# Seven-product up-projection of a gated MLP: the order of the products on TensorE, written out or left to the scheduler

## The chip, the cores and the metric

The kernel runs on one core of a Trainium2 chip, in one launch. Its time is device microseconds (us) of that core from start to end. Three runs of the kernel before gave 2424.66, 2425.37 and 2426.58 us; the median, 2425.37 us, is the time before. Five engines have instruction queues of their own and run side by side: TensorE (PE, matrix products into the accumulator PSUM), VectorE (DVE), ScalarE (ACT), GpSimd (POOL) and SyncE (SP, which here issues the DMA transfers). PSUM has eight banks; a product of 128 x 512 fp32 results fills one.

## What is computed

A two-layer decoder trunk on one sequence of 1024 positions and 1024 features. Each layer has a mixer (a gated recurrence with a state-space layer in layer 0, latent attention in layer 1) and then a gated MLP, which the change is about:

```python
def conv_ffn(hn, w_in, conv_w, conv_b, w_out):
    a, u = jnp.split(hn @ w_in, 2, axis=-1)       # w_in: 1024 x 5632
    a = causal depthwise convolution of width 3 over the positions of a, + conv_b
    return (jax.nn.silu(a) * u) @ w_out           # w_out: 2816 x 1024
```

`h = h + conv_ffn(rmsnorm(h))` is done once in each of the two layers. Everything is fp32; each fp32 matrix product is made of three products of halves (high x high, high x low, low x high).

## The kernel before

`ffn` works on 22 *pairs*: pair f is 128 columns of the `a` half and the 128 columns of the `u` half that belong to them. For one pair the product of `w_in` with the normed activations is a 2 x 2 block problem: two halves of the 1024 input features, two halves of the columns (u and a), two halves of the positions (`lo`, `hi`, 512 each). Instead of eight block products it makes seven, with sums of blocks before and after (Winograd's form). The seven are called by their weight operand: `a11`, `a12`, `s1`, `s2`, `s3`, `a22`, `s4`. A product is 12 matmuls of 128 x 512 (four steps of the inner dimension, three half products each, lines 161 to 163). The activations' blocks and their sums (`b11`, `b21`, `b22`, `bt1` to `bt4`) are made once per layer.

A pair has three PSUM banks. X takes `a11` and then, added to it, `a12`; Y takes `s2`, then `s3`, then `a22`, each added to what is there; Z takes `s1`, then `s4`. Between two products on one bank its contents are read: after `a11` ACT copies X to `p1` (line 895); after `s2` DVE writes `p16 = p1 + Y` (901); after `s3` DVE writes the `hi` half of the convolution's input, `ax = p1 + Y` (906), to which POOL adds `p5` (907); after `s1` ACT copies Z to `p5` (911); after `a22` DVE writes the `lo` half of `ax` (915), and then the convolution runs on DVE (1058, twice 1060) and SiLU on ACT (1061). The next product on that bank waits for the read. `tail` ends a pair: `p16 += Z` (922) and `ct[lo] *= X` (923) on DVE, `ct[hi] *= p16` on POOL (924), and a DMA of `ct` to DRAM. After all pairs `down` multiplies by `w_out`; its matmuls write tiles called `row`.

The weights of a pair come by DMA (846) into `raw` tiles (room for two pairs). POOL forms the sums `s1`, `s3`, `s2`, `s4` (877, 879, 881, 883), and `operand` splits each of the seven into a high half (ACT, line 129, `op`) and a low half (DVE, line 130, `op`). The `op` tiles are a ring of six; the text prepares each product three steps ahead (`LOOK`), so a slot is free again when the product six places earlier has ended.

Numbers of buffers matter below: `p16` has one, `p5` two, `p1` three, `ax` one, `ct` two. X, Y and Z of pairs 3 on are dealt from a ring of the eight banks; pair 2's Z is bank 0, which was pair 0's X.

What sets the order: each engine runs its own queue strictly in order. The order in the queues is made at build time by a scheduler that simulates the program and takes from the text, engine by engine, what it reckons to be ready first. So the list `steps` in the text is a proposal: products can be moved and interleaved on TensorE by the scheduler, and before the change they are.

Of the kernel before, what the change touches and what calls it, by code (L numbers as in the profile page):

```python
# [20 lines left out]
P = 128  # L21
# [35 lines left out]
class Trunk:  # L57
# [101 lines left out]
    def mm3(self, out, l, r, start, stop, **how):  # L159
        mm = self.nc.tensor.matmul  # L160
        mm(out, l[0], r[0], start=start, stop=False, **how)  # L161
        mm(out, l[0], r[1], start=False, stop=False, **how)  # L162
        mm(out, l[1], r[0], start=False, stop=stop, **how)  # L163
# [657 lines left out]
    def ffn(self, L, h, pool, final=None):  # L821
# [11 lines left out]
        KH = KD // 2  # L833
        quad = [P, 2, KH, HALF]
# [20 lines left out]
        def product(bank, w, x, start):  # L855

            for k in range(KH):
                self.mm3(
                    bank, [w[:, i, k] for i in range(2)], [v[:, k] for v in x],
                    start and k == 0, k == KH - 1, skip_group_check=not start,  # L860
                )

        class Pair:


            def __init__(s, f, r):
                s.f, s.r, s.op = f, r, {}
# [21 lines left out]

        def run(p, name):  # L890
# [7 lines left out]
            elif name == "s2":  # L898
                product(p.Y, o, B["t2"], True)
                p.p16 = piece("p16", 1)  # L900
                V.tensor_tensor(out=p.p16, in0=p.p1, in1=p.Y, op=ALU.add)  # L901
            elif name == "s3":
                product(p.Y, o, B["t3"], False)
                p.ax = pool.tile([P, S + 2], F32, tag="ax", name="ax", bufs=1)
                G.memset(p.ax[:, 0:2], 0.0)
                V.tensor_tensor(out=p.ax[:, 2 + HALF:], in0=p.p1, in1=p.Y, op=ALU.add)
                G.tensor_tensor(out=p.ax[:, 2 + HALF:], in0=p.ax[:, 2 + HALF:], in1=p.p5, op=ALU.add)
            elif name == "s1":
                product(p.Z, o, B["t1"], True)
                p.p5 = piece("p5", 2)  # L910
                ACT.activation(p.p5, p.Z, AF.Copy)  # L911
            elif name == "a22":
                product(p.Y, o, B["t4"], False)
                p.ct = pool.tile([P, S], F32, tag="ct", name="ct")
                V.tensor_tensor(out=p.ax[:, 2:2 + HALF], in0=p.p1, in1=p.Y, op=ALU.add)
                self.conv(p.ct, p.ax, taps, p.f, slice(0, S))
            else:
                product(p.Z, o, B["22"], False)
# [21 lines left out]
        def second_rows(t, q, ps):  # L940
            cols = slice(t * P, (t + 1) * P)
            if q == 0:
                f1 = B["f1"] = kn(piece("p16", 1))
# [54 lines left out]
        for p, y, z in zip(early, (5, 6, 7), (3, 4, 0)):  # L998
            p.banks = {"Y": y, "Z": z}
        steps = [(pairs[f], n) for f, n in (  # L1000
            (0, "s1"), (1, "s1"), (0, "s4"), (1, "s4"), (0, "s2"), (0, "s3"), (0, "a22"), (1, "s2"), (1, "s3"),
            (1, "a22"), (2, "s1"), (2, "s2"), (2, "s4"), (2, "s3"), (3, "a11"), (2, "a22"), (3, "s2"),
        )]
        order = ("a11", "s2", "a12", "s1", "s3", "a22", "s4")
# [565 lines left out]
```

## Time and profile before

| | us |
|---|---|
| median of three runs | 2425.37 |
| the profiled execution, its own time | 2429.82 |
| its span from the first to the last instruction | 2428.1 |
| up-projection stage of layer 0, first to last matmul of its products | 462.2 to 968.3 |
| the same of layer 1 | 1673.9 to 2180.0 |

The trace lists every instruction with its start, its duration and, in brackets, how long its engine had been idle before it and whose end it waited for. Times are us from the span's start. A matmul's listed duration is longer than the distance to the next one, because matmuls are pipelined; the pace of TensorE is read from starts. Tile names come without numbers: `au` is any of the banks X, Y, Z; `b` and `bt` are the blocks of the activations (`bt` belongs to `s1`, `s2`, `s3` and `a22`; `b` to `a11`, `a12` and `s4`); `p` is `p1`, `p5` or `p16`, told apart by line.

### The profile page before, as it was taken

The page shows a single profiled execution, that of the slowest core. Times are in us where ns is not written, and L with a number is a line of the kernel's source. Part 1 is how long each engine was busy: PE and PEld are TensorE (multiplying, and loading weights), DVE is VectorE, ACT ScalarE, POOL GpSimd, SP SyncE. Part 2 cuts the span into 40 slices and gives each one's busy share as a digit, 9 for nine tenths or more (in the row PEclk, how much of TensorE's full clock was granted, in tenths as well). Part 3 has the DMA queues.
Part 4 walks back from the last instruction along what each step waited for, and adds up shares of the span by engine and source line. Part 5 has one row for each costly group of instructions (what it writes and reads, how often), then busy time and mean ns, then how long its engine had stood idle before and what let it go on. Part 6 is the DMA issues. An engine that isn't in the chain of part 4 may idle for free.

```text
span 2428.1 us, 29242 instructions
## 1 busy us (share of the span) xinstructions
PE 2287.5 (94%) x10945; PEld 1862.1 (77%) x10945; DVE 1575.4 (65%) x2627; ACT 862.6 (36%) x1498; POOL 563.5 (23%) x509
## 2 busy tenths in 40 slices
PE   7999999989999999999989999999889999999997
PEld 6777878767777777888888888887667777778886
DVE  6878886775666666644467777847656666666435
ACT  4454553532332322311233555635322323223102
POOL 0465310233444342000001000001334443320000
PEclk9999999999999999999999999999999999999999
DMA  6333324122221223432301001431222222234211
GB/s 187 121 103 89 100 82 167 60 61 70 78 79 61 78 70 113 165 105 68 108 10 43 29 31 37 149 127 45 61 75 73 78 65 74 79 110 172 96 39 70
DMA packets 196309, 208.05 MB, mean 86 GB/s; under 512 B 28288, under 2 KB 152392, under 8 KB 195656
## 3 DMA queue, kind: packets, MB, share of 16 engines
q1 hardware_dynamic: 196168, 206.19, 26.0%
q8 instruction: 86, 1.41, 0.2%
q14 instruction: 55, 0.45, 0.1%
HBM read 165.39 MB, written 39.58 MB: 84 GB/s over the span
## 4 chain that ended last, share of the span: by engine, by line
PE 70%; DVE 13%; issue 7%; POOL 5%; DMA 3%; ACT 2%; SPq 0%; POOLq 0%; DVEq 0%; ACTq 0%
PE row L162 9%; PE row L163 9%; PE row L161 9%; PE au L161 7%; PE au L162 7%; PE au L163 7%; DVE op L130 2%; POOL ct L924 2%; POOL raw L879 2%; DMA raw<-in_ffn_w_in 1%; PE ptps L1468 1%; DVE wlo L130 1%; DVE p L901 1%; PE tt L162 1%; PE tt L163 1%
## 5 line engine op out<-in xcount | busy, mean ns | idle before, releaser
L161 PE MATMUL au<-bt,op 128*128 128x512 f32 x704 | 287.2, 408 | 60.6 <-DVE p L901 39.2
L129 ACT ACTIVATE op<-raw 128x512 fp32r<-128x512 f32 x260 | 162.7, 629 | 479.1 <-PE au L163 245.5
L129 ACT ACTIVATE whi<-raw 128x1024 fp32r<-128x1024 f32 (+4 forms) x143 | 143.4, 1004 | 410.5 <-PE row L163 273.5
L130 DVE TENSOR_TENSOR op<-raw,op 128x512 fp32r<-128x512 f32 x260 | 260.0, 1003 | 43.7 <-ACT op L129 38.2
L162 PE MATMUL au<-bt,op 128*128 128x512 f32 x704 | 282.2, 401 | 0.9 <-DVE bt L130 0.9
L162 PE MATMUL row<-wlo,g 128*128 128x512 f32 x704 | 275.7, 392 | 0.4 <-DVE wlo L130 0.2
L163 PE MATMUL au<-bt,op 128*128 128x512 f32 x704 | 275.3, 400 | 0.0
L163 PE MATMUL row<-whi,g 128*128 128x512 f32 x704 | 272.2, 390 | 0.0
L161 PE MATMUL row<-whi,g 128*128 128x512 f32 x704 | 265.7, 393 | 0.2 <-ACT whi L129 0.2
L130 DVE TENSOR_TENSOR wlo<-raw,whi 128x1024 fp32r<-128x1024 f32 (+4 forms) x143 | 173.2, 1212 | 109.8 <-ACT whi L129 107.8
L161 PE MATMUL au<-b,op 128*128 128x512 f32 x528 | 213.3, 404 | 28.9 <-ACT p L911 25.2
L1082 DVE TENSOR_TENSOR h<-h,row 128x512 f32<-128x512 f32 x192 | 129.5, 685 | 163.2 <-PE row L163 162.8
L161 PEld LDWEIGHTS au<-bt,op 128*128 128x128 f32 x704 | 134.8, 192 | 110.6 <-DVE p L901 55.0
L162 PE MATMUL au<-b,op 128*128 128x512 f32 x528 | 208.8, 395 | 0.0
L163 PE MATMUL au<-b,op 128*128 128x512 f32 x528 | 203.0, 396 | 0.0
L877 POOL TENSOR_TENSOR s<-raw 128x512 f32<-128x512 f32 x44 | 67.9, 1545 | 548.0 <-DMA raw<-in_ffn_w_in 420.7
L163 PEld LDWEIGHTS au<-bt,op 128*128 128x128 f32 x704 | 134.9, 192 | 32.2
L162 PEld LDWEIGHTS au<-bt,op 128*128 128x128 f32 x704 | 135.1, 192 | 31.8 <-DVE bt L130 1.5
L162 PEld LDWEIGHTS row<-wlo,g 128*128 128x128 f32 x704 | 132.2, 188 | 30.1 <-DVE wlo L130 2.1
L161 PEld LDWEIGHTS row<-whi,g 128*128 128x128 f32 x704 | 131.9, 188 | 30.1 <-ACT whi L129 1.5
L163 PEld LDWEIGHTS row<-whi,g 128*128 128x128 f32 x704 | 132.2, 188 | 29.7
L161 PEld LDWEIGHTS au<-b,op 128*128 128x128 f32 x528 | 99.5, 188 | 67.9 <-ACT p L911 41.3
(596 smaller groups left out, 4898.4 us busy)
## 6 DMA issues: line engine op xcount, KB each, us to landing
raw<-in_ffn_w_in SPq DMA_DIRECT2D x176, 256.0 KB, 3.3
g_dram<-ct SPq DMA_DIRECT2D x44, 512.0 KB, 4.0
raw<-in_ffn_w_out SPq DMA_DIRECT2D x44, 512.0 KB, 3.4
raw<-in_even_w_in SPq DMA_DIRECT2D x40, 512.0 KB, 3.9
gr<-g_dram SPq DMA_DIRECT2D x40, 512.0 KB, 4.5
h<-in_x SPq DMA_DIRECT2D x16, 512.0 KB, 10.4
raw<-in_even_w_out SPq DMA_DIRECT2D x16, 512.0 KB, 3.7
raw<-in_odd_w_out SPq DMA_DIRECT2D x16, 512.0 KB, 3.7
```

Of the source, the lines that this page charges most:

```text
L129: nc.scalar.activation(hi, src, AF.Copy)
L130: nc.vector.tensor_tensor(out=lo, in0=src, in1=hi.bitcast(F32), op=ALU.subtract)
L161: mm(out, l[0], r[0], start=start, stop=False, **how)
L162: mm(out, l[0], r[1], start=False, stop=False, **how)
L163: mm(out, l[1], r[0], start=False, stop=stop, **how)
L877: tt(out=s.s1, in0=p("a21"), in1=p("a22"), op=ALU.add)
L879: tt(out=p("s3"), in0=p("a11"), in1=p("a21"), op=ALU.subtract)
L901: V.tensor_tensor(out=p.p16, in0=p.p1, in1=p.Y, op=ALU.add)
L924: G.tensor_tensor(out=ct[:, hi], in0=ct[:, hi], in1=p.p16, op=ALU.mult)
L1082: nc.vector.tensor_tensor(out=part, in0=part, in1=acc, op=ALU.add)
L1468: nc.tensor.transpose(ps[:, w:w + P], pb[q][:, kk * P:(kk + 1) * P], self.ident)
```

## The change

Three edits, all in `ffn`. First, `product` is put under `issue_after(last)`: each product may be issued on TensorE only after the last matmul of the product before it in the text, so TensorE takes the products whole and in the order of `steps`. Second, that order is rewritten: `s1` and `s3` change places in the repeated `order` (now `a11 s2 a12 s3 s1 a22 s4`), and the list for the first pairs is mixed, so that between two products on one bank there is one on another. Third, `p16` gets a second buffer, and the `hi` half of the convolution's input is formed in another way: DVE writes `p1 + Y` to a tile of its own, `u3`, and POOL writes `ax = u3 + p5` once both are there (`second`), where before DVE wrote into `ax` and POOL added to it in place. The number of instructions and DMAs is the same.

```diff
--- before.py
+++ after.py
@@ -1,5 +1,5 @@
 import math
-from contextlib import ExitStack, contextmanager
+from contextlib import ExitStack, contextmanager, nullcontext
 
 import numpy as np
 
@@ -160,7 +160,7 @@
         mm = self.nc.tensor.matmul
         mm(out, l[0], r[0], start=start, stop=False, **how)
         mm(out, l[0], r[1], start=False, stop=False, **how)
-        mm(out, l[1], r[0], start=False, stop=stop, **how)
+        return mm(out, l[1], r[0], start=False, stop=stop, **how)
 
     def rstd(self, ss, n, width):
 
@@ -831,6 +831,7 @@
         g_row = self.gain(self.a["norm_ffn_g"][L:L + 1])
         g_dram = tc.dram_tile([NF, P, S], F32, name="g_dram")
         KH = KD // 2
+        last = []
         quad = [P, 2, KH, HALF]
         piece = lambda name, bufs: pool.tile([P, HALF], F32, tag=name, name=name, bufs=bufs)
         kn = lambda x: x.rearrange("p (k n) -> p k n", k=KH)
@@ -854,17 +855,19 @@
 
         def product(bank, w, x, start):
 
-            for k in range(KH):
-                self.mm3(
-                    bank, [w[:, i, k] for i in range(2)], [v[:, k] for v in x],
-                    start and k == 0, k == KH - 1, skip_group_check=not start,
-                )
+            with tc.issue_after(last[0].ins) if last else nullcontext():
+                for k in range(KH):
+                    mm = self.mm3(
+                        bank, [w[:, i, k] for i in range(2)], [v[:, k] for v in x],
+                        start and k == 0, k == KH - 1, skip_group_check=not start,
+                    )
+            last[:] = [mm]
 
         class Pair:
 
 
             def __init__(s, f, r):
-                s.f, s.r, s.op = f, r, {}
+                s.f, s.r, s.op, s.p5, s.u3 = f, r, {}, None, None
 
             def part(s, name):
                 j, i = {"a11": (0, 0), "a21": (0, 1), "a12": (1, 0), "a22": (1, 1), "s2": (0, 0), "s3": (0, 1), "s4": (1, 0)}[name]
@@ -887,6 +890,13 @@
 
         lo, hi = slice(0, HALF), slice(HALF, S)
 
+        def second(p):
+
+            if p.p5 is not None and p.u3 is not None:
+                p.ax = pool.tile([P, S + 2], F32, tag="ax", name="ax", bufs=1)
+                G.memset(p.ax[:, 0:2], 0.0)
+                G.tensor_tensor(out=p.ax[:, 2 + HALF:], in0=p.u3, in1=p.p5, op=ALU.add)
+
         def run(p, name):
             o = p.op.pop(name, None)
             if name == "a11":
@@ -897,18 +907,18 @@
                 product(p.X, o, B["21"], False)
             elif name == "s2":
                 product(p.Y, o, B["t2"], True)
-                p.p16 = piece("p16", 1)
+                p.p16 = piece("p16", 2)
                 V.tensor_tensor(out=p.p16, in0=p.p1, in1=p.Y, op=ALU.add)
             elif name == "s3":
                 product(p.Y, o, B["t3"], False)
-                p.ax = pool.tile([P, S + 2], F32, tag="ax", name="ax", bufs=1)
-                G.memset(p.ax[:, 0:2], 0.0)
-                V.tensor_tensor(out=p.ax[:, 2 + HALF:], in0=p.p1, in1=p.Y, op=ALU.add)
-                G.tensor_tensor(out=p.ax[:, 2 + HALF:], in0=p.ax[:, 2 + HALF:], in1=p.p5, op=ALU.add)
+                p.u3 = piece("u3", 1)
+                V.tensor_tensor(out=p.u3, in0=p.p1, in1=p.Y, op=ALU.add)
+                second(p)
             elif name == "s1":
                 product(p.Z, o, B["t1"], True)
                 p.p5 = piece("p5", 2)
                 ACT.activation(p.p5, p.Z, AF.Copy)
+                second(p)
             elif name == "a22":
                 product(p.Y, o, B["t4"], False)
                 p.ct = pool.tile([P, S], F32, tag="ct", name="ct")
@@ -940,7 +950,7 @@
         def second_rows(t, q, ps):
             cols = slice(t * P, (t + 1) * P)
             if q == 0:
-                f1 = B["f1"] = kn(piece("p16", 1))
+                f1 = B["f1"] = kn(piece("p16", 2))
                 V.tensor_tensor(out=f1, in0=kn(ps), in1=f11[:, :, cols], op=ALU.subtract)
                 return
             V.tensor_tensor(out=f2[:, :, cols], in0=kn(ps), in1=B["f1"], op=ALU.subtract)
@@ -998,10 +1008,10 @@
         for p, y, z in zip(early, (5, 6, 7), (3, 4, 0)):
             p.banks = {"Y": y, "Z": z}
         steps = [(pairs[f], n) for f, n in (
-            (0, "s1"), (1, "s1"), (0, "s4"), (1, "s4"), (0, "s2"), (0, "s3"), (0, "a22"), (1, "s2"), (1, "s3"),
-            (1, "a22"), (2, "s1"), (2, "s2"), (2, "s4"), (2, "s3"), (3, "a11"), (2, "a22"), (3, "s2"),
+            (0, "s1"), (1, "s1"), (0, "s4"), (0, "s2"), (1, "s4"), (0, "s3"), (1, "s2"), (0, "a22"), (1, "s3"),
+            (2, "s1"), (1, "a22"), (2, "s2"), (2, "s4"), (2, "s3"), (3, "a11"), (2, "a22"), (3, "s2"),
         )]
-        order = ("a11", "s2", "a12", "s1", "s3", "a22", "s4")
+        order = ("a11", "s2", "a12", "s3", "s1", "a22", "s4")
         steps += [(pairs[3], n) for n in order[2:]] + [(p, n) for p in pairs[4:] for n in order]
 
         def prep(p, name):
```

What the scheduler makes of it is seen in three places of layer 0's repeated part. Line numbers in `ffn` are 1 to 10 higher after the change.

TensorE before, one turn of the repeated part; the first matmul of each product (or of a piece of one). `au` with a number is one use of a bank: 5270 is Y of a pair n, 4992 is Y of pair n-1, 5170 is Z of pair n-1, 5249 is X of pair n and 5388 is X of pair n+1.

```order
L161 MATMUL au_4992<-bt3_4498,op_4986 128x512
...
L161 MATMUL au_5270<-bt2_4107,op_5205 128x512
...
L161 MATMUL au_5170<-bt1_4106,op_5107 128x512
...
L161 MATMUL au_4992<-bt4_4501,op_5007 128x512
...
L163 MATMUL au_5170<-bt1_4106,op_5107 128x512
...
L161 MATMUL au_5170<-b22_4108,op_5161 128x512
...
L161 MATMUL au_5249<-b21_4102,op_5226 128x512
...
L161 MATMUL au_5388<-b11_4101,op_5324 128x512
```

In turn: `s3` of n-1, `s2` of n, `s1` of n-1 with `a22` of n-1 inside it, `s4` of n-1 right behind that `s1` on the same bank, `a12` of n, `a11` of n+1.

TensorE after, one turn; X, Y and Z of one pair are 5258, 5276 and 5333.

```order
L161 MATMUL au_5258<-b11_4101,op_5189 128x512
...
L161 MATMUL au_5276<-bt2_4107,op_5211 128x512
...
L161 MATMUL au_5258<-b21_4102,op_5232 128x512
...
L161 MATMUL au_5276<-bt3_4498,op_5252 128x512
...
L161 MATMUL au_5333<-bt1_4106,op_5273 128x512
...
L161 MATMUL au_5276<-bt4_4501,op_5291 128x512
...
L161 MATMUL au_5333<-b22_4108,op_5306 128x512
```

All seven products of the turn belong to one pair, whole, and no two neighbours share a bank.

GpSimd before, one turn; `raw` 5303 and 5306 are the weights of pair n+1, 5442 and 5445 those of pair n+2, `ct_5359` is pair n's product-to-be.

```order
L877 TENSOR_TENSOR s1_5545<-raw_5442,raw_5445 128x512
L883 TENSOR_TENSOR raw_5306<-raw_5306,raw_5303 128x4x128
L905 MEMSET ax_5479 128x2
L879 TENSOR_TENSOR raw_5442<-raw_5442 128x4x128
L924 TENSOR_TENSOR ct_5359<-ct_5359,p16_5283 128x512
L881 TENSOR_TENSOR raw_5442<-s1_5545,raw_5442 128x4x128
L907 TENSOR_TENSOR ax_5479<-ax_5479,p5_5461 128x512
```

GpSimd after, one turn; pair n has `ax_5348`, `raw` 5309 and 5312 are those of pair n+2.

```order
L880 TENSOR_TENSOR s1_5395<-raw_5309,raw_5312 128x512
L882 TENSOR_TENSOR raw_5309<-raw_5309 128x4x128
L886 TENSOR_TENSOR raw_5172<-raw_5172,raw_5169 128x4x128
L898 TENSOR_TENSOR ax_5348<-u3_5327,p5_5346 128x512
L897 MEMSET ax_5488 128x2
L934 TENSOR_TENSOR ct_5366<-ct_5366,p16_5289 128x512
L884 TENSOR_TENSOR raw_5309<-s1_5395,raw_5309 128x4x128
```

Before, `ct *= p16` (924) stands behind `s1` and `s3` of a pair whose weights have just been loaded (877, 879). After, it (934) stands ahead of these two (880, 882), behind the adding up of `ax` and the clearing of its two first columns.

VectorE before, from the `lo` half of pair n's `ax` (5340) on; `p16_5422` is that of the pair behind it.

```order
L915 TENSOR_TENSOR ax_5340<-p1_5262,au_5270 128x512
L130 TENSOR_TENSOR op_5403<-raw_5164,op_5403 128x512
L1058 TENSOR_SCALAR ct_5359<-ax_5340,taps_4096 128x1024
L1060 SCALAR_TENSOR_TENSOR ct_5359<-ax_5340,taps_4096,ct_5359 128x1024
L130 TENSOR_TENSOR op_5504<-raw_5306,op_5504 128x512
L1060 SCALAR_TENSOR_TENSOR ct_5359<-ax_5340,taps_4096,ct_5359 128x1024
L130 TENSOR_TENSOR op_5602<-raw_5442,op_5602 128x512
L923 TENSOR_TENSOR ct_5359<-ct_5359,au_5249 128x512
L130 TENSOR_TENSOR op_5563<-raw_5306,op_5563 128x512
L130 TENSOR_TENSOR op_5578<-raw_5306,op_5578 128x512
L901 TENSOR_TENSOR p16_5422<-p1_5401,au_5409 128x512
L922 TENSOR_TENSOR p16_5422<-p16_5422,au_5448 128x512
```

VectorE after, from the convolution of pair n (`ct_5366`) on; `p16_5289` is pair n's and `p16_5429` the next one's.

```order
L925 TENSOR_TENSOR ax_5348<-p1_5271,au_5276 128x512
L130 TENSOR_TENSOR op_5413<-s1_5255,op_5413 128x512
L1068 TENSOR_SCALAR ct_5366<-ax_5348,taps_4096 128x1024
L1070 SCALAR_TENSOR_TENSOR ct_5366<-ax_5348,taps_4096,ct_5366 128x1024
L932 TENSOR_TENSOR p16_5289<-p16_5289,au_5333 128x512
L130 TENSOR_TENSOR op_5431<-raw_5172,op_5431 128x512
L1070 SCALAR_TENSOR_TENSOR ct_5366<-ax_5348,taps_4096,ct_5366 128x1024
L130 TENSOR_TENSOR op_5446<-raw_5172,op_5446 128x512
L933 TENSOR_TENSOR ct_5366<-ct_5366,au_5258 128x512
L911 TENSOR_TENSOR p16_5429<-p1_5411,au_5416 128x512
L130 TENSOR_TENSOR op_5469<-raw_5309,op_5469 128x512
L130 TENSOR_TENSOR op_5491<-raw_5309,op_5491 128x512
```

Before, `p16` and its `+= Z` stand together. After, `p16 += Z` (932) has moved up into the convolution, and the writing of the next `p16` (911) stands behind `ct *= X` (933) of the pair before.

## Rows read from the trace of the kernel before

**Rows 1.** The page's part 1: busy us (share of the span) and instructions by engine.

```profile
PE 2287.5 (94%) x10945; PEld 1862.1 (77%) x10945; DVE 1575.4 (65%) x2627; ACT 862.6 (36%) x1498; POOL 563.5 (23%) x509
```

**Rows 2.** Stretches: length, busy us (matmuls) by engine, granted clock, DMA.

```profile
core 0: us, PE busy (x) PEld busy (x) DVE busy (x) ACT busy (x) POOL busy (x), PEclk, DMA share, GB/s
510.70:523.20 12.50, 5.83 (x24) 4.43 (x24) 7.42 (x8) 2.32 (x3) 4.85 (x5) 0.85 0.28 81
561.60:586.10 24.50, 19.99 (x72) 15.43 (x72) 12.18 (x16) 4.68 (x8) 7.03 (x6) 0.86 0.24 68
586.10:932.60 346.50, 321.47 (x1344) 250.20 (x1344) 215.25 (x242) 102.69 (x163) 146.70 (x112) 1.00 0.23 75
932.60:955.00 22.40, 18.97 (x76) 13.90 (x76) 15.29 (x18) 7.55 (x11) 6.52 (x6) 1.00 0.30 111
1725.10:1736.10 11.00, 5.83 (x24) 4.43 (x24) 6.91 (x8) 3.60 (x4) 4.36 (x5) 0.93 0.19 55
1775.40:1798.70 23.30, 18.78 (x72) 14.48 (x72) 12.22 (x16) 4.68 (x8) 7.04 (x6) 0.93 0.24 71
1798.70:2144.30 345.60, 320.58 (x1344) 249.53 (x1344) 215.45 (x242) 102.70 (x163) 146.78 (x112) 1.00 0.23 75
2144.30:2165.50 21.20, 17.73 (x72) 13.19 (x72) 13.80 (x16) 6.50 (x10) 5.96 (x5) 1.00 0.31 119
```

**Rows 3.** Who waited for whom: us in total, times, longest us.

```profile
PE au L161 <- DVE p L901: 39.2, 36, 3.9
...
DVE p L901 <- POOL ct L924: 46.2, 40, 1.8
...
PE au L161 <- ACT p L911: 25.2, 37, 0.7
```

**Rows 4.** Timeline of TensorE in one turn: start, duration, idle before.

```profile
702.93 0.39 PE L163 MATMUL au<-b,op 128*128 128x512 f32 x1
704.23 0.50 PE L161 MATMUL au<-bt,op 128*128 128x512 f32 x1 [0.92 <-DVE p L901]
704.57 0.39 PE L162 MATMUL au<-bt,op 128*128 128x512 f32 x1
...
715.27 0.39 PE L163 MATMUL au<-bt,op 128*128 128x512 f32 x1
716.34 0.50 PE L161 MATMUL au<-b,op 128*128 128x512 f32 x1 [0.69 <-ACT p L911]
```

**Rows 5.** Timeline of GpSimd in the same turn.

```profile
700.06 1.71 POOL L879 TENSOR_TENSOR raw<-raw 128x512 f32<-128x512 f32 x1
701.72 1.74 POOL L924 TENSOR_TENSOR ct<-ct,p 128x512 f32<-128x512 f32 x1
```

**Rows 6.** Instructions on tile `p`: ns min/median/max, first and last start.

```profile
L911 ACT ACTIVATE p<-au x44: 579/597/601, 492.4 to 2161.6; 128x512 f32<-128x512 f32 x44
L901 DVE TENSOR_TENSOR p<-p,au x44: 675/689/691, 504.0 to 2167.9; 128x512 f32<-128x512 f32 x44
```

**Rows 7.** Instructions on tile `op`, VectorE and ScalarE: ns min/median/max.

```profile
L130 DVE TENSOR_TENSOR op<-raw,op x260: 678/693/1847, 451.6 to 2159.9; 128x512 fp32r<-128x512 f32 x130
L129 ACT ACTIVATE op<-raw x260: 610/632/637, 450.9 to 2159.3; 128x512 fp32r<-128x512 f32 x130
```

**Rows 8.** Timeline of all engines around pair 0's tail, layer 0.

```profile
514.26 0.69 DVE L915 TENSOR_TENSOR ax<-p,au 128x512 f32<-128x512 f32 x1 [2.88 <-PE au L163]
...
517.44 0.81 DVE L1058 TENSOR_SCALAR ct<-ax,taps 128x1024 f32<-128x1024 f32 x1 [0.99 <-POOL ax L907]
518.28 1.29 DVE L1060 SCALAR_TENSOR_TENSOR ct<-ax,taps,ct 128x1024 f32<-128x1024 f32 x1
...
521.40 1.06 ACT L1061 ACTIVATE ct<-ct 128x1024 f32<-128x1024 f32 x1 [4.20 <-DVE ct L1060]
522.49 0.69 DVE L923 TENSOR_TENSOR ct<-ct,au 128x512 f32<-128x512 f32 x1 [1.12 <-ACT ct L1061]
...
523.23 0.80 PE L161 MATMUL au<-bt,op 128*128 128x512 f32 x1 [6.70 <-DVE ct L923]
```

**Rows 9.** Timeline of VectorE at the end of layer 0's stage.

```profile
953.73 1.23 DVE L130 TENSOR_TENSOR wlo<-raw,whi 128x1024 fp32r<-128x1024 f32 x1 [1.38 <-PE au L163]
```

**Rows 10.** The page's DMA issues: KB each, median us to landing.

```profile
raw<-in_ffn_w_in SPq DMA_DIRECT2D x176, 256.0 KB, 3.3
```

## Prediction, made before the changed kernel ran

> **What bounds the kernel now.** I read the page's busy shares first, then the waits, then the stretches of the two up-projection stages, then one turn in the timeline. TensorE is busy 94% of the span [rows 1], so only what makes it wait, or run at half clock, can be won. In the list of waits two belong to the products: `au` matmuls wait 39.2 us for `p16` (36 times) and 25.2 us for `p5` (37 times) [rows 3].
>
> One turn shows both. The matmuls between 704.57 and 715.27 are 46 starts apart, 10.70 / 46 = 0.2326 us each [rows 4]; a product of 12 is 2.79 us, a pair of seven 19.54 us. The first stall: the last start before it is 702.93, the next is 704.23, 1.30 us instead of 0.23, and the one behind that comes 0.34 later instead of 0.23, so 1.18 us are lost. The second (715.27 to 716.34, again with a slow restart) costs 0.95 us. Together 2.13 us a pair, and 19.54 + 2.13 = 21.67; the long stretch of layer 0 has 1344 matmuls, 16 pairs, in 346.5 us, 21.66 us each [rows 2]. So these two stalls are all that TensorE loses there, at a granted clock of 1.00.
>
> Why they wait differs. The second is two products on one bank with nothing between: `s4` stands right behind `s1`, and ACT's copy of Z (0.60 us, [rows 6]) lies between them. The first is not that: `s3` stands six products behind its `s2`. It waits for `p16`, which waits for its only buffer, which POOL reads in `ct *= p16`: that wait of DVE for POOL is 46.2 us in 40 times [rows 3], and POOL does the 1.74 us of `ct *= p16` behind the 1.71 us of an `s3` sum [rows 5], whose weights have just come in. So it is a ring from the weights' landing over POOL and DVE to TensorE, and the buffer closes it.
>
> **The change, part by part.** Time lost against 0.2326 us a matmul, by stretch [rows 2]:
>
> - Repeated part: 346.5 - 1344 x 0.2326 = 33.9 us in layer 0, 345.6 - 312.6 = 33.0 in layer 1.
> - The 72 matmuls before it: 24.5 - 16.75 = 7.75 and 23.3 - 16.75 = 6.55 us; it is the same wait for `p16` at its longest (3.9 us, [rows 3]) and the half clock after it (granted 0.86 and 0.93).
> - The end: 22.4 - 76 x 0.2326 = 4.7 and 21.2 - 16.75 = 4.45 us.
> - The wait for bank 0 (pair 2's Z, pair 0's X) at the start: 12.5 - 5.58 = 6.9 and 11.0 - 5.58 = 5.4 us.
>
> *The repeated part.* To see what is late next I lay the new queues over a turn of 19.54 us, with 0 at the start of `a11` of pair n. A result is there 0.16 us after its product's last slot (0.39 of duration less 0.23). Durations: DVE reads of a bank 0.69, ACT reads 0.60 [rows 6]; split 0.63 on ACT and 0.69 on DVE [rows 7]; convolution 0.81 + 1.29 + 1.29, SiLU 1.06 [rows 8].
>
> DVE's queue: `a22` of n-1 ends at -2.63; `ax` to -1.94, a low split to -1.25, 0.81 to -0.44, 1.29 to 0.85, `p16 += Z` to 1.54, a split to 2.23, 1.29 to 3.52. SiLU then stands behind ACT's copy of X (`a11` ends 2.95, copy to 3.55) and a high split, to 4.18; SiLU to 5.24, `ct *= X` to 5.93, and then `p16` of n (`s2` ended at 5.74) to 6.62. `s3` starts at 8.37: 1.75 us spare. `u3` is read from 11.32 to 12.01, `a22` starts at 13.95: 1.94 spare. `p5` is copied from 14.11 to 14.71, `s4` starts at 16.74: 2.0 spare. `p16`'s buffer was last used two pairs earlier and is free at about 7.0 of the turn before; its wait on POOL goes.
>
> The operands: each split waits for the slot of the product six places ahead, is done within 2.5 us of it, and its product starts five products (14 us) after it. POOL: `ct *= p16` 5.24 to 6.98, then the sum `s2`, then the sums of the pair after next once their weights are there. The last of these is issued when the low split of `s4` of n is done (4.9) and lands 3.3 us later [rows 10], at 8.2; two sums of 1.7 us end at 11.6, before the `s4` sum, which cannot start before 12.7 (low split of `a12`) and is wanted by ACT at 23.1. Nothing in the turn is late. So both stalls go and I take the floor: 66.9 us won.
>
> *The rest.* The 72 matmuls: same ring, same answer, 14.3 us won. Bank 0: the list still has `s1` of pair 2 one product after `a22` of pair 0. The chain behind that `a22` is read, split, 0.81, 1.29, the read to `u3` (new in it), a split, 1.29, SiLU, `ct *= X`: 0.69 x 5 + 3.39 + 1.06 = 7.9 us. `s3` of pair 1 covers 2.79; 8.1 - 2.8 = 5.3 us and the restart stay lost. Before, DVE waited 2.5 us for POOL's part of `ax` (514.95 to 517.44, [rows 8]), which is now done by then. Against 6.9 and 5.4 that wins 1.5 and 0. The end: `w_out`'s first low half now stands in DVE's queue behind `p16 += Z` of the last pair: 0.16 + 0.69 + 1.23 [rows 9] and a restart, 2.2 us lost against 4.7 and 4.45: 4.75 won. POOL's add of `ax` costs as before, off the path; DVE writes `u3` for `ax`, same size.
>
> Unknown: the first products of each layer also keep the text's order, among transposes that stay free. A product that waits there now holds up the others; the nearest price is one wait for a `p5` or split, up to 3 us a layer either way. I take 0, and keep plus or minus 3 for the range.
>
> Sum: 66.9 + 14.3 + 1.5 + 4.75 = 87.4 us. The profiled execution took 2429.8; 2342.4. The median lies 4.45 us lower: 2338.
>
> **A rule that speaks against it.** The low splits of operands take 0.69 us in the median but up to 1.85 [rows 7], while the reads of a bank into `p16` stay between 0.675 and 0.691 in all 44 cases [rows 6]. The Trainium skill, "SBUF — State Buffer", section "Who interferes with whom", says that a VectorE instruction with two SBUF inputs contends with a GpSimd instruction that reads SBUF, and whoever comes first holds the shared ports to its end. The rows agree: the split reads two SBUF tiles, the read of a bank only one. By that rule the same POOL work in a turn two us shorter catches more splits; that is the first rival. By the laid-out turn POOL is idle while the convolution runs (it waits to clear `ax`), which is why I don't take it.
>
> **Rivals.**
>
> *1. Slowed splits make `p16` late (12%).* In the chain to `p16` stand three low splits. If POOL catches all three, each costs 1.85 - 0.69 = 1.16 us more: the last convolution step ends at 5.84, the split behind it at 7.69, `ct *= X` at 8.38, `p16` at 9.07, 0.70 us after `s3` should start; with the restart 0.85 us a pair. For 19 pairs a layer 2 x 19 x 0.85 = 32 us: 2370. For it: such splits are there. Against: POOL's idle time at that place.
>
> *2. Another ring keeps the period (5%).* The change does not do what it says if what holds the 21.66 us is the weights' ring and not the buffer: then the spare moves and only the ends are won, 1.5 + 4.75 and perhaps as much again: 2425 - 6 to 2425 - 12, say 2416. For it: POOL's sums wait for DMA. Against: by the laid-out turn that ring has nearly 10 us spare (worked out in rival 3).
>
> *3. Slower: the fixed order makes TensorE wait for weights (4%).* Before, TensorE could be given other products ahead of a late one; now one late split stops all. The place is the `s4` sum on POOL, behind two sums that wait for the weights' landing. The spare is 1.1 us ahead of that sum and 23.1 - 12.7 - 1.7 = 8.7 behind it, to ACT's high split: 9.8 us. A landing later than 3.3 + 9.8 = 13.1 us would cost each pair the excess, and from 13.1 + 2.13 = 15.2 us the repeated part is slower than before. At 17 us it is 3.9 us a pair, 2338 + 2 x 19 x 3.9 = 2486. Against it: a median landing of 3.3 us [rows 10].
>
> **How the numbers follow.** The forecast, 2338 us, has 79%; its own range is 2328 (the 3 us a layer and a little of the bank wait) to 2350 (some pairs with a short wait for `p16`). The range for 8 in 10 reaches up to rival 1: 2327 to 2370. A measurement of this kernel tells about 0.2%, 5 us, from no change. Faster: 79 + 12 + 3 of rival 2 = 94%; the same: 2%; slower: 4%.
>
> **What would show it.** In the trace after: starts of `au` matmuls 0.23 us apart through a whole pair, and a period of 19.5 us; no wait of `au` for `p16`, `u3` or `p5` in the repeated part; DVE's wait for POOL at `p16` gone; one wait of about 5 us for `ct *= X` left at the start of each stage and one of 2 us at its end. Wrong if a wait of `s3` for `p16` comes back in each pair (rival 1, with splits of over 1.5 us just ahead of it), if the period stays over 21 us (rival 2), or if TensorE waits for splits (rival 3).

## The result and the profile after

The changed kernel takes 2328.32 us (median of four runs, 2326.70 to 2330.02), the kernel before, run beside it, 2425.01 (2424.12 to 2426.58). The ratio is 0.960, 95% interval 0.9584 to 0.9617: 96.7 us less. In the two profiled executions the span went from 2428.1 to 2326.6 us.

Busy time by engine, from the page of after (us, share of the span, instructions), answers to [rows 1]:

```profile
PE 2253.3 (97%) x10945; PEld 1857.8 (80%) x10945; DVE 1541.0 (66%) x2627; ACT 860.9 (37%) x1498; POOL 535.1 (23%) x509
```

The stretches of after that answer to [rows 2]: length, busy us and count by engine, granted clock, DMA. The first ends with the wait for bank 0 of layer 0, the second is what comes right behind it; then come the 72 matmuls ahead of the repeated part, the repeated part, and the end of the stage; the last but one is the repeated part of layer 1, the last the end of that stage. A count (x) also holds the one or two matmuls that began ahead of the stretch and reach into it.

```profile
506.40:517.35 10.95, 5.00 (x23) 3.73 (x21) 9.65 (x12) 2.46 (x4) 7.66 (x6) 0.95 0.16 48
517.35:534.40 17.05, 17.05 (x62) 13.62 (x63) 9.22 (x10) 4.18 (x7) 7.42 (x7) 0.83 0.18 62
534.40:550.80 16.40, 16.40 (x72) 13.21 (x72) 11.56 (x16) 5.08 (x8) 8.96 (x8) 1.00 0.30 97
550.80:863.40 312.60, 312.60 (x1344) 251.97 (x1343) 200.83 (x241) 101.57 (x160) 131.75 (x114) 1.00 0.26 83
888.00:912.40 24.40, 23.15 (x99) 18.19 (x98) 16.72 (x19) 9.33 (x11) 3.57 (x3) 1.00 0.49 169
...
1696.90:2009.50 312.60, 312.60 (x1351) 252.64 (x1350) 203.16 (x245) 101.57 (x160) 133.74 (x114) 1.00 0.26 84
...
2050.00:2071.90 21.90, 20.55 (x88) 16.07 (x88) 14.30 (x17) 8.68 (x10) 3.56 (x3) 1.00 0.47 169
```

About as many matmuls as took 346.5 us (1344) now take 312.6, a little under 0.233 us each, and TensorE is busy for all of it. The list of waits of TensorE (total, times, longest) has no line for `p16` (911), `u3` (915) or `p5` (920) any more; what is left in the stages is the wait for bank 0, which answers to [rows 3], and two short ones where `down` begins:

```profile
PE au L161 <- DVE ct L933: 12.4, 2, 6.4
...
PE row L161 <- DVE p L932: 1.3, 2, 0.7
PE row L162 <- DVE wlo L130: 1.3, 2, 0.6
```

The wait for bank 0 in layer 0, on the timeline:

```profile
517.32 0.79 PE L161 MATMUL au<-bt,op 128*128 128x512 f32 x1 [5.95 <-DVE ct L933]
```

One turn of after, first TensorE where `a12` ends and `s3` (on `bt`) begins, then VectorE, from the `lo` half of `ax` to the read into `p16`, and GpSimd's `ct *= p16`; start, duration, idle before. They answer to [rows 4] and [rows 5]:

```profile
701.45 0.39 PE L163 MATMUL au<-b,op 128*128 128x512 f32 x1
701.68 0.40 PE L161 MATMUL au<-bt,op 128*128 128x512 f32 x1
701.92 0.39 PE L162 MATMUL au<-bt,op 128*128 128x512 f32 x1
```

```profile
690.72 0.69 DVE L925 TENSOR_TENSOR ax<-p,au 128x512 f32<-128x512 f32 x1 [0.27 <-PE au L163]
...
698.38 0.69 DVE L933 TENSOR_TENSOR ct<-ct,au 128x512 f32<-128x512 f32 x1 [0.26 <-ACT ct L1071]
699.09 0.69 DVE L911 TENSOR_TENSOR p<-p,au 128x512 f32<-128x512 f32 x1
...
710.26 0.69 DVE L925 TENSOR_TENSOR ax<-p,au 128x512 f32<-128x512 f32 x1 [0.26 <-PE au L163]
```

```profile
698.43 1.30 POOL L934 TENSOR_TENSOR ct<-ct,p 128x512 f32<-128x512 f32 x1 [1.64 <-ACT ct L1071]
```

`s3` starts 0.23 us behind `a12`; `p16` was read by 699.78, 1.9 us earlier. The period is 710.26 - 690.72 = 19.54 us.

Where the span's 101.5 us lie, by the first product matmul of each layer (462.20 and 1673.87 before, 459.36 and 1623.44 after): 2.8 us ahead of layer 0's stage, where TensorE does the same instructions in the same order; 1211.67 - 1164.08 = 47.6 from there to layer 1's first product; 754.23 - 703.16 = 51.1 from there to the end.

### The profile page after: what moved, and what is told of

Read it like the earlier page. It is cut to its first block, busy times and chain, and to the rows that moved or that the text cites. A ratio compares the mean times of both kernels' runs of the same rounds, so it can differ in the third digit from the quotient of the medians.

```text
span 2326.6 us, 29393 instructions
## 1 busy us (share of the span) xinstructions
PE 2253.3 (97%) x10945; PEld 1857.8 (80%) x10945; DVE 1541.0 (66%) x2627; ACT 860.9 (37%) x1498; POOL 535.1 (23%) x509
## 5 line engine op out<-in xcount | busy, mean ns | idle before, releaser
L130 DVE TENSOR_TENSOR op<-raw,op 128x512 fp32r<-128x512 f32 x260 | 229.8, 886 | 213.3 <-ACT op L129 211.4
L880 POOL TENSOR_TENSOR s<-raw 128x512 f32<-128x512 f32 x44 | 60.0, 1365 | 260.2 <-DMA raw<-in_ffn_w_in 229.0
```

The costliest lines, as they stand in the source:

```text
L130: nc.vector.tensor_tensor(out=lo, in0=src, in1=hi.bitcast(F32), op=ALU.subtract)
L880: tt(out=s.s1, in0=p("a21"), in1=p("a22"), op=ALU.add)
```

## The experiments

Each was timed beside the kernel before, whose median was between 2427.1 and 2428.9 us in the three sessions (2425.0 beside the changed kernel), so that 2 to 4 us between two rows of the table say little. They ask which of the three edits won the time, and what the waits were made of.

| pin | text | p16 | u3 | median us | ratio to before, interval |
|---|---|---|---|---|---|
| yes | new | 2 | yes | 2328.3 (after) | 0.960, 0.9584 to 0.9617 |
| no | old | 2 | no | 2315.4 | 0.954, 0.9524 to 0.9556 |
| no | new | 2 | no | 2315.4 | 0.953, 0.9517 to 0.9545 |
| no | new | 2 | yes | 2319.3 | 0.956, 0.9542 to 0.9570 |
| yes | new | 2 | no | 2328.6 | 0.959, 0.9581 to 0.9607 |
| yes | new | 1 | yes | 2373.5 | 0.978, 0.9763 to 0.9792 |
| no | new | 1 | yes | 2392.8 | 0.986, 0.9845 to 0.9872 |
| yes | old | 1 | no | 2409.0 | 0.993, 0.9910 to 0.9940 |
| yes | old turn | 2 | yes | 2375.6 | 0.978, 0.9764 to 0.9797 |

### 1. The second p16 buffer alone

```diff
-                p.p16 = piece("p16", 1)
+                p.p16 = piece("p16", 2)
-                f1 = B["f1"] = kn(piece("p16", 1))
+                f1 = B["f1"] = kn(piece("p16", 2))
```

> The kernel before with one edit: p16 gets two buffers; nothing pins the order, and Y is still added after the GpSimd product. Theory A (the single p16 buffer is what closes the ring in the repeated part, and the order only follows from it): with two buffers the scheduler's own order already keeps s1, s3, s4 and a22 apart, so both stalls of a pair (1.18 and 0.95 us) go and the time is 2330 to 2345 us. Rival B (the written order is what removes the stalls): s3 no longer waits for p16, 38 x 1.18 = 45 us less at most, but the bank waits stay: about 2380 us; if the bank wait only grows in place of the other, 2400 to 2425 us.

2315.36 us: theory A, and better than it said. One number in the kernel before gives more than the whole change; the interval of its ratio lies below that of after. Its repeated parts run without a gap, as those of after (stretches as above, layer 0 and 1):

```profile
586.10:898.70 312.60, 312.60 (x1342) 251.89 (x1341) 210.20 (x239) 101.54 (x160) 127.77 (x107) 1.00 0.26 85
1697.00:2009.60 312.60, 312.60 (x1349) 252.36 (x1348) 216.67 (x243) 101.61 (x163) 141.28 (x117) 1.00 0.25 81
```

The scheduler's own order in a turn is now `s1`, two matmuls of `a11`, `s3`, eight more, `s4`, two more, one of `s2`, `a22`, the rest of `s2`, `a12`: no two products on one bank stand next to each other. So `s4` right behind `s1`, the second stall of before, was not a habit of the scheduler's; with two `p16` it goes together with the first. Why the scheduler put the two side by side with one `p16` was not looked into. On VectorE the read into `p16` now comes between two convolution steps of the pair before, ahead of that pair's tail:

```profile
691.26 1.28 DVE L1060 SCALAR_TENSOR_TENSOR ct<-ax,taps,ct 128x1024 f32<-128x1024 f32 x1
692.47 0.68 DVE L901 TENSOR_TENSOR p<-p,au 128x512 f32<-128x512 f32 x1
...
696.08 0.69 DVE L923 TENSOR_TENSOR ct<-ct,au 128x512 f32<-128x512 f32 x1 [1.13 <-ACT ct L1061]
```

### 2. After with one p16

The edit is the first one's, the other way round, in the kernel after.

> The kernel after with p16 back at one buffer; same order on TensorE. Theory A (by the laid-out turn p16 is released about 7.0 us into the turn, written by 7.7 us, and s3 needs it at 8.4 us, so in the written order one buffer is just enough): 2328 to 2334 us. Rival B (the one buffer closes the ring over GpSimd in this order too): its wait of about 1.2 us a pair comes back, 38 x 1.2 = 46 us: about 2374 us.

2373.49 us is rival B's number, but by luck: rival B is wrong. The repeated parts are whole; the time lies in the first pairs (the stretches with 157 and 158 matmuls in 64 us):

```profile
506.00:570.00 64.00, 43.18 (x157) 33.60 (x156) 35.29 (x37) 12.36 (x18) 25.71 (x20) 0.82 0.20 66
600.00:912.60 312.60, 312.60 (x1344) 251.99 (x1343) 199.19 (x240) 101.56 (x160) 127.11 (x110) 1.00 0.25 81
1692.00:1756.00 64.00, 42.60 (x158) 33.24 (x157) 33.82 (x39) 14.06 (x20) 24.62 (x19) 0.84 0.20 65
1780.00:2092.60 312.60, 312.60 (x1351) 252.63 (x1350) 201.03 (x242) 102.18 (x161) 127.48 (x110) 1.00 0.25 81
```

In the first pairs TensorE waits three times a layer for `p16`, in layer 0:

```profile
520.96 0.80 PE L161 MATMUL au<-bt,op 128*128 128x512 f32 x1 [9.34 <-DVE p L911]
543.01 0.79 PE L161 MATMUL au<-bt,op 128*128 128x512 f32 x1 [5.42 <-DVE p L911]
564.97 0.80 PE L161 MATMUL au<-bt,op 128*128 128x512 f32 x1 [6.06 <-DVE p L911]
```

These are `s3` of pairs 1, 2 and 3. The list has `s3` of pair 1 right behind `a22` of pair 0, and those of pairs 2 and 3 two products behind the `a22` of the pair before, where the repeated part has four products between them; a single `p16` is held until that earlier pair's tail is done. In the repeated part the read into `p16` comes in time. These rows show GpSimd's `ct *= p16`, which here stands ahead of the weight sums, VectorE's read, and TensorE at the start of `s3`:

```profile
701.32 1.29 POOL L934 TENSOR_TENSOR ct<-ct,p 128x512 f32<-128x512 f32 x1 [1.65 <-ACT ct L1071]
...
703.30 0.68 DVE L911 TENSOR_TENSOR p<-p,au 128x512 f32<-128x512 f32 x1
...
704.58 0.39 PE L161 MATMUL au<-bt,op 128*128 128x512 f32 x1
```

`s3` starts at 704.58 and `p16` is read by 703.98: 0.6 us spare, so one buffer is just enough. The written and pinned order by itself does remove both stalls of a pair there. Only the last pair of each stage waits for `p16` again, 0.83 and 0.81 us.

### 3. The pin alone, with the text and the buffer of before

```diff
+            with tc.issue_after(last[0].ins) if last else nullcontext():
```

> The kernel before with the pin alone: the order of products is the text's of before (a11 s2 a12 s1 s3 a22 s4 in the repeated part, in which s3 and a22 on bank Y stand next to each other), one p16, no u3. Theory A (order and separation are the point, a pin by itself gives nothing): s3's wait for p16 and a wait of a22 or s4 for the release of the bank before it stay, about 1 to 2 us a pair: 2375 to 2430 us. Rival B (a fixed order alone is enough, whatever it is): about 2330 us.

2409.01 us is in theory A's range, but the pin alone gives 18 us, and of the two waits that theory A kept only one stays in the repeated part. `a22` waits behind `s3`, its neighbour on bank Y, in nearly every pair (40 times); the wait for `p16` is left only at the starts (8 times):

```profile
PE au L161 <- DVE ax L909: 31.8, 40, 0.9
PE au L161 <- DVE p L904: 31.3, 8, 7.1
```

### 4. After without the pin

```diff
-            with tc.issue_after(last[0].ins) if last else nullcontext():
+            with nullcontext():
```

> The kernel after with the pin alone taken out: two p16 buffers, the sum u3, and the new text, whose order the scheduler is free to change. Theory A (buffers and u3 open the ring, and the scheduler keeps products on one bank apart by itself): within 5 us of the kernel after, 2326 to 2334 us. Rival B (without the pin the scheduler puts two products on one bank side by side): one bank wait of about 0.95 us a pair, 38 x 0.95 = 36 us: about 2365 us.

2319.31 us, 9 less than after: theory A's mechanism, and below its range, since the pin costs time with this list. The repeated parts are the same. In the profile it takes 1157.4 us from the first product of layer 0 to that of layer 1, against 1164.1, and 701.4 from there to the end, against 703.2. The wait for bank 0 is 0.94 us in layer 0 and gone in layer 1, where after has 5.95 and 6.43. The first 408 product matmuls of the stage, all that come before the repeated part of before, take 107.8 us in layer 0 against 113.8 in after. In layer 1 they take 111.0 against 111.1, and 12 transposes (1.2 us) stand among them which after has ahead of them: so 6.0 and 1.3 us are won. In layer 1 other waits stand in place of the one for bank 0, the longest 2.74 us for ACT's copy of X, which after doesn't have.

### 5. After without u3

```diff
-                p.u3 = piece("u3", 1)
-                V.tensor_tensor(out=p.u3, in0=p.p1, in1=p.Y, op=ALU.add)
+                p.ax = pool.tile([P, S + 2], F32, tag="ax", name="ax", bufs=1)
+                G.memset(p.ax[:, 0:2], 0.0)
+                V.tensor_tensor(out=p.ax[:, 2 + HALF:], in0=p.p1, in1=p.Y, op=ALU.add)
+                p.u3 = p.ax[:, 2 + HALF:]
```

> The kernel after without u3: VectorE writes p1 + Y into the second half of ax at s3, as the kernel before did, and GpSimd adds p5 there. The pin, the new order and two p16 stay. Theory A (ax is free some 8 us before s3's result is there, so u3 decouples nothing in the written order): within 3 us of the kernel after, 2325 to 2331 us. Rival B (VectorE then has to wait for ax, and a22, which follows on the same bank, waits with it): about 1 us a pair, 38 us more, 2366 us.

2328.57 us: theory A. `u3` brings nothing in the written order. The waits for bank 0 are even shorter without it, 5.11 and 4.69 us.

### 6. Pair 2's s1 later in the list

```diff
-            (2, "s1"), (1, "a22"), (2, "s2"), (2, "s4"), (2, "s3"), (3, "a11"), (2, "a22"), (3, "s2"),
+            (2, "s2"), (1, "a22"), (3, "a11"), (2, "s3"), (2, "s1"), (2, "a22"), (3, "s2"), (2, "s4"),
```

(Pair 3's weights and sums are asked for at the steps that this list needs.)

> The kernel after with another list for the first pairs: pair 2's s1, which needs pair 0's X bank, stands four products later (a11 of pair 3, s2 and s3 of pair 2 and a22 of pair 1 come before it), and the loads are issued at the step that this list needs. Theory A (the wait for ct *= X, 5.95 and 6.43 us in the two layers, and the half clock behind it are a matter of the list's order at one place): 2310 to 2317 us. Rival B (the first pairs' products all hang on VectorE's queue, so the wait only moves to another product): 2325 to 2332 us.

2319.48 us (2315.53 to 2320.48), 9 less than after: theory A's mechanism, 2.5 us short of its range. The wait for `ct *= X` is gone; in its place stand 0.40 us for `u3` and 0.94 for `p16` (0.17 and 0.94 in layer 1). With this list the pinned kernel is as fast as the one without a pin (experiment 4).

### 7. The pin only from the 16th product on

```diff
-        last = []
+        last, free = [], [6 + 9]
-            with tc.issue_after(last[0].ins) if last else nullcontext():
+            with tc.issue_after(last[0].ins) if last and free[0] <= 0 else nullcontext():
+            free[0] -= 1
```

> The kernel after with the pin lifted for the first 15 products of each layer's stage (those of the first pairs); from there on the order is pinned as in the kernel after. Theory A (what the pin costs, 9 us against the kernel without it, lies at the start of the stages, where TensorE may not go round a product that waits): 2317 to 2323 us. Rival B (the pin costs at its other places, or the wait for bank 0 stays because the products that could fill it are later than the 15th): 2325 to 2332 us.

2342.68 us, 14 more than after: both theories missed. The wait for bank 0 grew to 8.84 and 9.73 us. Left free, the scheduler puts `s3` of pair 1 ahead of `a22` of pair 0, on which `ct *= X` hangs, and the pinned `s1` of pair 2 then stands right behind that `a22`, with nothing left between them. VectorE's read into `u3`, which waits 3.29 us for GpSimd to be done with the only `u3`, stands there ahead of the read behind that `a22`. A pin from the middle on fixes the waiting product and lets the one it waits for slip.

### 8. The new text with one p16 and no pin

The edits of 2 and 4 together.

> The kernel after without the pin and with one p16: of the change only the new text and u3 are left. It completes the square of pin (yes, no) and p16 buffers (two, one), of which three corners took 2328, 2373 and 2319 us. Theory A (either the pinned order or the second buffer opens the ring in the repeated part, and where neither is there the scheduler falls back into the order with the two stalls): 2415 to 2430 us. Rival B (the new text alone leads the scheduler to the good order): 2370 us or less.

2392.75 us, between the two. The turn is 20.52 us long (from 588.18 to 608.70); the scheduler finds another order (`s1 s2 s4 a11 s3`, two matmuls of `a12`, `a22`, the rest of `a12`), in which the first matmul of `a12` waits for its operand in each pair:

```profile
PE au L161 <- ACT op L129: 28.8, 39, 1.5
```

So the fall back into the old order that theory A expected is not a rule, and one `p16` does not force that order. Why this operand is late was not followed up.

### 9. The old turn, pinned, with two p16

```diff
-        order = ("a11", "s2", "a12", "s3", "s1", "a22", "s4")
+        order = ("a11", "s2", "a12", "s1", "s3", "a22", "s4")
```

> The kernel after with one thing back: in the repeated turn the pinned order is the one of the kernel before's text (a11 s2 a12 s1 s3 a22 s4), in which s3 and a22, both on bank Y, stand next to each other. Two p16, u3 and the pin stay. Theory A (with the order pinned the product on another bank between two on one bank is worth the read of the bank, about 0.9 us a pair): 0.78 + 0.11 us of wait and restart in each of some 38 pairs, 34 us more than the kernel after, 2358 to 2368 us. Rival B (with two p16 the separation in the text doesn't matter): 2325 to 2333 us.

2375.60 us: theory A, dearer than it said. Of the list of waits, and two neighbouring waits on the timeline:

```profile
PE au L161 <- DVE u L915: 29.2, 36, 1.4
PE au L161 <- DVE ct L933: 12.4, 2, 6.4
```

```profile
571.04 0.50 PE L161 MATMUL au<-bt,op 128*128 128x512 f32 x1 [0.78 <-DVE u L915]
591.67 0.50 PE L161 MATMUL au<-bt,op 128*128 128x512 f32 x1 [0.78 <-DVE u L915]
```

The period is 20.63 us here and 20.52 in layer 1, where after needs 19.56 and 19.46 (16 pairs in 313.0 and 311.4 us, from start to start), so a neighbour on the same bank costs about 1.07 us a pair, not 0.9: the idle of 0.78 counts from a matmul's modelled end, 0.16 behind its slot. Over 38 pairs that is about 40 us, which the stages show (469.7 and 467.1 against 450.1 and 445.6 us, 41 in all). The medians differ by 47 us, but by 43 when each is taken beside its own kernel before (53.3 against 96.7 us less), so little is left. In the two profiles the time from stage to stage is 5 us longer here; this profile shows stretches there at a granted clock of 0.98 that ran at 1.00 in after. That was not settled.

### 10. ct *= p16 on VectorE, in the kernel before

```diff
-            G.tensor_tensor(out=ct[:, hi], in0=ct[:, hi], in1=p.p16, op=ALU.mult)
+            V.tensor_tensor(out=ct[:, hi], in0=ct[:, hi], in1=p.p16, op=ALU.mult)
```

> The kernel before with ct *= p16 on VectorE instead of GpSimd; one p16, no pin, the order on TensorE as before. Theory A (what keeps the one p16 taken is GpSimd, which does ct *= p16 only behind the sums of the next weights): the buffer is free right behind ct *= X, s3's wait of 1.18 us a pair and the longer one ahead of it go, s4's stays: 2370 to 2385 us. Rival B (p16 is late because VectorE's own queue is late, and the multiplication adds 0.7 us or more a pair to that queue): 2415 to 2435 us.

2442.16 us, ratio 1.005 (1.0035 to 1.0065): theory A fell, and the time is 7 us above rival B's range. VectorE no longer waits for GpSimd at `p16`, and TensorE waits longer for it, 1.35 us of idle a pair in place of 0.92. First one turn of VectorE in the kernel before, then the same in this one (x2: two instructions in one row):

```profile
691.70 0.69 DVE L915 TENSOR_TENSOR ax<-p,au 128x512 f32<-128x512 f32 x1 [4.71 <-PE au L163]
...
698.18 0.69 DVE L923 TENSOR_TENSOR ct<-ct,au 128x512 f32<-128x512 f32 x1 [0.53 <-ACT ct L1061]
698.78 1.82 DVE L130 TENSOR_TENSOR op<-raw,op 128x512 fp32r<-128x512 f32 x1
700.76 1.55 DVE L130 TENSOR_TENSOR op<-raw,op 128x512 fp32r<-128x512 f32 x1 [0.15 <-ACT op L129]
703.49 0.69 DVE L901 TENSOR_TENSOR p<-p,au 128x512 f32<-128x512 f32 x1 [1.18 <-POOL ct L924]
...
713.38 0.69 DVE L915 TENSOR_TENSOR ax<-p,au 128x512 f32<-128x512 f32 x1 [4.69 <-PE au L163]
```

```profile
690.91 0.69 DVE L915 TENSOR_TENSOR ax<-p,au 128x512 f32<-128x512 f32 x1 [4.69 <-PE au L163]
...
697.40 0.69 DVE L923 TENSOR_TENSOR ct<-ct,au 128x512 f32<-128x512 f32 x1 [0.52 <-ACT ct L1061]
698.00 1.82 DVE L924 TENSOR_TENSOR ct<-ct,p 128x512 f32<-128x512 f32 x1
699.75 3.48 DVE L130 TENSOR_TENSOR op<-raw,op 128x512 fp32r<-128x512 f32 x2
703.15 0.68 DVE L901 TENSOR_TENSOR p<-p,au 128x512 f32<-128x512 f32 x1
...
713.05 0.69 DVE L915 TENSOR_TENSOR ax<-p,au 128x512 f32<-128x512 f32 x1 [4.71 <-PE au L163]
```

The reader can close the ring from these rows. Before, from the `ax` read behind `a22` to the end of the read into `p16` it is 704.18 - 691.70 = 12.48 us; from there over `s3`, `s2`, two matmuls of `s1` and `a22` to the next `ax` read 713.38 - 704.18 = 9.20: together 21.68, the period. Here it is 12.92 + 9.22 = 22.14. With the written order and one buffer (experiment 2) the first part is 703.98 - 693.59 = 10.39, in all 19.6, and TensorE's own 19.54 us decide.

What this shows is limited. In the kernel before, 1.18 of the 12.48 us are VectorE's wait for GpSimd; without it the ring would take 21.68 - 1.18 = 20.50 us, and TensorE with its second stall needs 19.54 + 0.95 = 20.49. So by these rows GpSimd's late `ct *= p16` can be the whole of the first stall. The experiment took that wait away, but put the multiplication's 1.82 us into VectorE's queue instead, and the ring grew. It shows that the move gains nothing, not that the wait was harmless. `ct *= p16` ahead of the sums on GpSimd, with one `p16` and nothing else changed, was not run; in experiment 2, where it stands there and the order is another one too, `p16` is in time.

GpSimd works on sums from 697.99 to 702.67, and the multiplication and both splits beside them take 1.82 and 1.74 us each, where a split by itself takes 0.69 [rows 7]. The Trainium skill, "SBUF — State Buffer", section "Who interferes with whom", says that a VectorE instruction with two SBUF inputs contends with GpSimd's reads; the rows agree. The read into `p16`, with one input from PSUM, stays at 0.675 to 0.691 in all 44 cases before [rows 6], among them the one above at 703.49, which runs beside a GpSimd sum from 703.41 to 704.68.

### 11. Two p16 and the new text, neither pin nor u3

The edits of 4 and 5 together.

> The kernel after without the pin and without u3: two p16 and the new text, whose order the scheduler is free to change. It stands between the kernel with two p16 alone (2315 us) and the one with two p16, u3 and the new text (2319 us). Theory A (the 4 us between them come from u3): 2313 to 2317 us. Rival B (they come from the text, which the scheduler follows where nothing else decides): 2318 to 2322 us.

2315.37 us: theory A. From the first product to the last it takes 442.2 and 442.3 us, with `u3` 444.5 and 445.8. With `u3` five matmuls of `down` (1.2 us) stand in each of these stretches, so some 3.5 us are left for `u3` without the pin; the intervals of the ratios still touch. In the trace of experiment 4 VectorE waits 3.49 us in the first pairs (at 514.83) until GpSimd is done with the only `u3`. The text's order costs nothing that the times show when nothing pins it: 2315.37 us here, 2315.36 in experiment 1.

## Why the prediction was right, and where its terms were off

The forecast was 2338 us, 2328.3 were measured: 87.4 us won by the forecast and 96.7 in fact. The measurement lies 1.3 us inside the lower end of the range of 2327 to 2370, so the mechanism of the repeated part came out well and the sum only just.

*Repeated part, 33.9 + 33.0: right.* Nothing is late. From start to start the 1344 matmuls take 313.0 and 311.4 us, so 33.5 + 34.2 us are won. The margin laid out for `p16` was 1.75 us; it is 1.9. Experiments 1, 2 and 9 show what carries it: either the second buffer or the order with a neighbour on another bank removes both stalls here. I had laid the second stall (`s4` behind `s1`) to the written order alone; experiment 1 shows that the buffer, without any pin, removes it too. With a pin, the order must be the new one (experiment 9: about 40 us).

*The 72 matmuls, 7.75 + 6.55: right.* In the 16.40 us 71 matmuls start, which is the floor, and layer 1 has no wait there either. But the second buffer, not the order, wins this term: without it the changed kernel is 45 us slower, some 42 of them in the first pairs (experiment 2), far more than the 14.3 that I had put on that wait.

*Bank 0, 1.5 + 0: too small, and the term that failed most.* The wait came where it was forecast, 5.95 and 6.43 us of idle against 5.3, with 2.6 us more behind it in layer 0 (62 matmuls in 17.05 us at a granted clock of 0.83, a part of it at 1.2 instead of 2.4 GHz). But from the first product to the end of that wait the stage took 61.0 and 62.2 us before, and 58.0 and 56.7 after: 3.0 and 5.5 us won, of which 1.2 in layer 1 are 12 transposes that after has ahead of its first product; so 3.0 + 4.3. I had read the row of the wait alone and left the products ahead of it at "plus or minus 3 us a layer, taken 0". In layer 1 a wait of 2.75 us for ACT's copy of X (895) was before among them, and after has none; without the pin it is there (2.74 us in experiment 4). What comes behind the wait, up to the repeated part, loses 2.6 and 1.5 us; before, up to the 72 matmuls, it lost 2.1 and 3.0: 1.0 us more won. So 8.3 us were won where 1.5 were forecast, and these 6.8 are most of the 9.3 that the forecast lacked. I also took the 2.5 us from 514.95 to 517.44 before [rows 8] for a wait of VectorE for GpSimd; only 0.99 of it is, and the rest is a split of 1.46 us.

*The end, 4.75: small but right.* The two waits where `down` begins are 0.61 and 0.63 us in layer 0 instead of the one of 2.2 that I forecast. In 24.40 us 98 matmuls start, 24.40 - 98 x 0.2326 = 1.6 us lost, and 21.90 - 87 x 0.2326 = 1.7 in layer 1: 4.7 + 4.45 - 3.3 = 5.9 won.

The terms as measured: 67.7 + 14.3 + 8.3 + 5.9 = 96.2. The two spans that they are read from differ by 101.5; 2.8 of that lies ahead of the first stage, and some 2.5 us were not put down to a place. Between the medians it is 96.7.

*"A ring from the weights' landing over POOL and DVE to TensorE": right on the buffer, in part open on the rest.* The second buffer opens the ring (experiment 1). The ring runs from `a22` over VectorE's convolution and tail to `p16` and back over `s3`, and it stays closed with `ct *= p16` off GpSimd (experiment 10): there VectorE is never idle between `ct *= X` and the read into `p16`, so no landing holds it either. GpSimd lengthens the ring by slowing the splits that stand in it, and in the kernel before by its late `ct *= p16`, 1.18 us. How much of the first stall each of the two made before is not shown.

*What I did not see:* that the pin costs 9 us with this list (experiment 4). The profiles put 7.3 of them at the starts, 6.0 in layer 0 and 1.3 in layer 1, where TensorE may not go round a product that waits; the rest was not found. With another list for the first pairs the pin costs nothing that the times show (experiment 6).

*The rivals.* Rival 1's slowed splits are real in the ring of before, but did not make `p16` late after: 1.9 us spare in the turn shown, and no wait for it. Rivals 2 and 3 are out: the period is 19.54, and no product of the repeated part waits for a split.

## What to carry to other kernels

Ahead of writing out an order, try a second buffer for the tile that closes the ring: here one number was worth 112 us, the whole change 97. To see what would be left of a ring, add it up from start to start (12.48 + 9.20 = 21.68 here) and take each wait out of the sum. The last releaser of a wait tells what ended it, not what a change there is worth: in experiment 10, taking the work off that engine put it into another queue of the same ring, and the kernel was 13 us slower. A pin is paid where the work is irregular: check each product at a stage's start for the one it waits on, since nothing can go round it (9 us here, won back by another list), and a pin on only a part of the list can be worse (14 us more in experiment 7).

## What was not expected of the hardware

The convolution's first step takes 0.81 us in all 44 cases before (802 to 814 ns), but in 2 of 44 after it takes 1.78 and 1.76 us, in pair 0 at the start of each stage. In layer 0 GpSimd was in a sum from 509.35 to 511.14:

```profile
509.90 1.78 DVE L1068 TENSOR_SCALAR ct<-ax,taps 128x1024 f32<-128x1024 f32 x1
```

These are the only two of the 44 that ran beside a GpSimd instruction on tensors. The chain to `ct *= X`, on which bank 0 hangs, is about 1 us longer for it; the forecast had this step at 0.81. And two neighbouring products on one bank cost 0.95 us where ACT reads the bank between them (0.60 us of copy) and about 1.07 where VectorE does (0.69): in these two cases the longer read is the dearer one.
